# Shifting SBUF places to multiples of 256 bytes in a twelve-stage network kernel

## Chip, core and metric

The kernel runs on one core of a Trainium2 chip. The metric is device time in microseconds (us) of one execution; lower is better. A difference of about 0.3% (8 us) is the least that a measurement of this kernel can tell from none.

## The reference

A residual stream `x` of 256 tokens by 1024 features passes through twelve blocks in float32. In short:

```python
for i in range(2):                                  # first block
    x = x + 0.5 * swiglu(rmsnorm(x, g), w_in, w_out)
    x = x + (chunked_sgu(h) if i == 0 else pool_mixer(h))
    x = x + 0.5 * swiglu(rmsnorm(x, g), w_in, w_out)
x = rmsnorm(x, final_norm)
x = x + gt1 * rms_norm(attention(h) @ w_o)          # second block
x = x + gt2 * rms_norm(moe_ffn(h2))                 # 32 experts, top 4
x = x + rms_norm(merged @ w_out)                    # third block: attention + state space
x = x + rms_norm(memory_cross_attention(h))
x = x + rms_norm(conv_ffn(h))

def moe_ffn(h, ...):                                # for every expert e with its tokens
    hid = xb @ w_mlp1[e] + b_mlp1[e]                # 1024 x 2048 weights, 8 MiB
    act = clipped_swiglu(hid)
    y   = act @ w_mlp2[e] + b_mlp2[e]               # 1024 x 1024 weights, 4 MiB
```

The 32 experts' weights are 12 MiB each, 384 MiB together.

## The kernel before

**Dense stages.** A weight column block of 128 outputs is loaded by one DMA of 1 MiB (128 partitions, 8 KiB each) into a place `raw` (pool `rawp`, ten places, `slot` and `raw`, lines 311 to 318). ACT casts it to a float32r tile `hi` (line 181), DVE subtracts to get `lo` (line 182); `parts` (line 327) takes the two from a ring of places of 8 KiB in the pools `splitp` and `splitr`. The inputs are split the same way (`input`, `ahi`/`alo` and others). `mm3` (lines 198 to 200) then makes three products for every 128 inputs: hi with hi, hi with lo, lo with hi, each with a 128x128 stationary operand and 256 moving columns. These are the "split products".

**Experts' stage** (`moe`, line 1270 on). The weights are not split. `weights` (line 1299) issues twelve DMAs of 1 MiB for each expert on SP's queue (`load`, line 1294): eight parts of `w_mlp1`, four of `w_mlp2`, each 128 rows of 8192 bytes. They go round a cycle of sixteen places (line 1285): seven `raw`, four `wb` from the pool `p3` (`own`, line 1281), the two places that are lent to it, `input` and the residual `xT` itself (line 1284), then three `raw`. So a load begins as soon as the product that last read its place is done, and up to sixteen loads run ahead. `xT` is saved to DRAM first (`kept`, line 1342) and read back at the end. `xe` holds the rows of the tokens that an expert gets; its place is lent to one load of the first expert. First layer products are at lines 1516 and 1548 (stationary `xe`, moving a weight place), second layer at 1590.

**How places are laid out.** A pool is a stretch of SBUF that opens on top of the pools still open, on the left or the right end; what a pool holds is laid out in it in order, at multiples of 32 bytes. `shift(pool, n)` (line 90) only reserves n bytes that nothing uses; it issues no instruction. Where a new pool covers what an earlier one held, the first writer of each new tile waits for the last reader of every old tile it overlaps. As allocated in the kernel before (start address modulo 256, and modulo 512 where it matters): `xT`, `raw`, `input` at 224; `wb` and `xe` at 32; the `hi`/`lo` places at 32; the moving operands of the split products at 224, which is 192 behind the stationary ones modulo 512, or 320 ahead. `wb` stands exactly on the four places that `splitp` held before the stage, and `b1`, `quarter`, `halves` and `xe0` exactly on the fifth.

**Order of issue.** Instructions are put in order by a scheduler that goes by priorities and by when operands are ready; inside `in_order` blocks PE follows the program. SP works through its DMAs strictly in that order, so a DMA that waits for its place holds up all that stand behind it. The last products ahead of the experts belong to a side job that is interleaved with attention and the experts (`mem.key(6)`, line 1188).

Of the kernel before, what the change touches and what calls it, by code (L numbers as in the profile page):

```python
# [41 lines left out]
class Net:  # L42
    def __init__(self, ctx, tc, I):
        self.ctx, self.tc, self.nc, self.I = ctx, tc, tc.nc, I
        self.uid = 0
        pool = lambda name, bufs, **kw: ctx.enter_context(tc.tile_pool(name=name, bufs=bufs, **kw))
        self.const = pool("const", 1)
        self.psum = pool("psum", 8, space=PSUM)
        self.small = pool("small", 2)
        self.rawp = pool("rawp", 10, reuse_waits="tile")  # L50
        self.inputs = pool("inputs", 2, reuse_waits="tile")
        self.ring_size, self.ring_scope, self.right_scope, self.latest = None, None, None, ()
        self.rings(8)
        nc = self.nc
        self.ident = self.const.tile([P, P], F32, name="ident")
        make_identity(nc, self.ident)
        self.ones = self.const.tile([P, 1], F32, name="ones")
        nc.vector.memset(self.ones, 1.0)
        self.mhalf = self.const.tile([P, 4], F32, name="mhalf")
        nc.vector.memset(self.mhalf, -0.5)  # L60
        self.sc = self.const.tile([P, KT], F32, name="sc")
        self.xT = self.const.tile([P, KT, T], F32, name="xT")
        self.new_inputs()

# [4 lines left out]
    def rings(self, split, right=0, left=0):  # L69

        if self.right_scope is not None:
            self.right_scope.close()
        self.right_scope = ExitStack()
        if self.ring_size != split:
            if self.ring_scope is not None:
                self.ring_scope.close()
            self.ring_size = split
            self.ring_scope = ExitStack()
            if split:
                self.splitp = self.ring_scope.enter_context(self.tc.tile_pool(name=self.nm("splitp"), bufs=split, reuse_waits="tile"))  # L80
        self.turn_of = [self.splitp] * split
        self.shifts = {}
        for n, side in ((right, "right"), (left, "left")):
            if n:
                more = self.right_scope.enter_context(self.tc.tile_pool(name=self.nm("splitr"), bufs=n, reuse_waits="tile", side=side))
                self.turn_of += [more] * n
                if side == "right":
                    self.shifts[more] = 448

    def shift(self, pool, n):  # L90

# [1178 lines left out]
    def moe(self, V, mod, router, w1, w2, b2, nxt, ahead, mem):  # L1270
# [7 lines left out]
        top, p0, p6 = (pool(name, side="right") for name in ("mot", "mo0", "mo6"))  # L1278
        p3, pb = pool("mo3", 4), pool("mob")

        own = lambda: p3.tile([P, 2048], F32, tag="wb", name=self.nm("wb"))


# [1593 lines left out]
```

## Time and profile before

| what | value |
|---|---|
| median of 3 runs | 2651.24 us (2647.99 to 2656.15) |
| the profiled execution | 2649.92 us |
| its span, first to last instruction | 2648.2 us |
| mean granted TensorE clock | 0.95 |
| PE, DVE, ACT, POOL busy | 91%, 51%, 35%, 10% |
| DMA over the span | 718.30 MB, mean 271 GB/s |

The profile is of one execution; the times of its rows add up to the span, and 1.7 us lie around it. Busy PE time is modelled from pipelined matmuls, so a busy PE is not PE at its peak; counts of matmuls per stretch (the x behind a busy time) tell its pace. "DMA" is the mean busy share of 16 DMA engines. Times in rows count from the start of the span.

### The profile page before, as it was taken

The page shows a single profiled execution, that of the slowest core. Times are in us where ns is not written, and L with a number is a line of the kernel's source. Part 1 is how long each engine was busy: PE and PEld are TensorE (multiplying, and loading weights), DVE is VectorE, ACT ScalarE, POOL GpSimd, SP SyncE. Part 2 cuts the span into 40 slices and gives each one's busy share as a digit, 9 for nine tenths or more (in the row PEclk, how much of TensorE's full clock was granted, in tenths as well). Part 3 has the DMA queues.
Part 4 walks back from the last instruction along what each step waited for, and adds up shares of the span by engine and source line. Part 5 has one row for each costly group of instructions (what it writes and reads, how often), then busy time and mean ns, then how long its engine had stood idle before and what let it go on. Part 6 is the DMA issues. An engine that isn't in the chain of part 4 may idle for free. (4 is left out here: it accounts for less than half of the span.)

```text
span 2648.2 us, 42809 instructions
## 1 busy us (share of the span) xinstructions
PE 2416.1 (91%) x17207; PEld 1833.3 (69%) x17207; DVE 1339.3 (51%) x2778; ACT 915.4 (35%) x1531; POOL 254.3 (10%) x444
## 2 busy tenths in 40 slices
PE   7999999999999998999988988888787688999998
PEld 7998999999989998783333433233232156899997
DVE  5556767577787766832112111111111059766875
ACT  4446454454454445531101101001010043555653
POOL 0011000110021003120000000000000027111000
PEclk9999999999999999989989999899898788999998
DMA  8965555676647652469999999999999973444640
GB/s 247 329 196 193 185 204 192 220 263 231 216 158 248 223 168 94 158 250 391 419 414 417 416 416 419 420 419 419 420 419 420 420 286 112 160 165 139 222 144 17
DMA packets 274405, 718.30 MB, mean 271 GB/s; under 512 B 15055, under 2 KB 179387, under 8 KB 223643
## 3 DMA queue, kind: packets, MB, share of 16 engines
q1 hardware_dynamic: 269658, 705.73, 71.3%
q0 software_dynamic: 4544, 9.80, 1.1%
q8 instruction: 136, 2.23, 0.3%
q14 instruction: 67, 0.54, 0.1%
HBM read 704.89 MB, written 10.59 MB: 270 GB/s over the span
## 5 line engine op out<-in xcount | busy, mean ns | idle before, releaser
L200 PE MATMUL b<-input,hi 128*128 128x256 f32 x2392 | 671.6, 281 | 16.2 <-DVE hi L182 16.1
L198 PE MATMUL b<-input,hi 128*128 128x256 f32 x2392 | 675.5, 282 | 6.4 <-ACT input L210 5.1
L182 DVE TENSOR_TENSOR hi<-raw,hi 128x1024 fp32r<-128x1024 f32 (+3 forms) x517 | 605.8, 1183 | 146.4 <-ACT hi L181 145.5
L199 PE MATMUL b<-input,hi 128*128 128x256 f32 x2392 | 670.6, 280 | 3.7 <-DVE input L211 2.4
L181 ACT CAST hi<-raw 128x1024 fp32r<-128x1024 f32 (+3 forms) x517 | 509.0, 1002 | 469.4 <-PE b L200 408.2
L198 PEld LDWEIGHTS b<-input,hi 128*128 128x128 f32 x2392 | 456.4, 191 | 20.1 <-ACT hi L181 7.2
L200 PEld LDWEIGHTS b<-input,hi 128*128 128x128 f32 x2392 | 455.4, 190 | 18.9 <-DVE hi L182 18.8
L199 PEld LDWEIGHTS b<-input,hi 128*128 128x128 f32 x2392 | 456.0, 191 | 5.8 <-DVE input L211 4.5
L1497 DVE TENSOR_SCALAR g<-b 128x256 f32<-128x256 f32 x48 | 20.3, 423 | 588.4 <-PE b L1516 327.7
L198 PE MATMUL b<-ahi,hi 128*128 128x256 f32 x1072 | 299.2, 280 | 2.2 <-ACT ahi L181 2.2
L199 PE MATMUL b<-alo,hi 128*128 128x256 f32 x1072 | 298.0, 278 | 3.3 <-DVE alo L660 1.9
L200 PE MATMUL b<-ahi,hi 128*128 128x256 f32 x1072 | 297.5, 278 | 0.8 <-DVE hi L182 0.8
L199 PEld LDWEIGHTS b<-alo,hi 128*128 128x128 f32 x1072 | 202.4, 189 | 4.4 <-DVE alo L182 2.2
L198 PEld LDWEIGHTS b<-ahi,hi 128*128 128x128 f32 x1072 | 202.0, 189 | 3.6 <-ACT ahi L181 3.6
L200 PEld LDWEIGHTS b<-ahi,hi 128*128 128x128 f32 x1072 | 202.0, 189 | 1.0 <-DVE hi L182 1.0
L1500 ACT ACTIVATE sg<-g 128x256 f32<-128x256 f32 x48 | 20.0, 417 | 516.8 <-DVE g L1497 516.8
L1548 PE MATMUL b<-raw,xe 128*64 128x512 f32 x600 | 140.9, 607 | 10.2 <-DMA raw<-in_w_mlp_dram 10.1
L1516 PE MATMUL b<-raw,xe 128*32 128x512 f32 x784 | 107.9, 660 | 32.9 <-DMA raw<-in_w_mlp_dram 32.9
L1597 ACT COPY y<-b 64x512 f32<-64x512 f32 x68 | 39.4, 580 | 253.9 <-PE b L1590 246.1
L474 DVE TENSOR_TENSOR t<-b,rb 128x256 f32<-128x256 f32 x88 | 37.1, 422 | 151.7 <-PE b L200 151.6
L1548 PEld LDWEIGHTS b<-raw,xe 128*64 128x64 f32 x600 | 39.8, 138 | 104.8 <-issue 73.8
L1516 PEld LDWEIGHTS b<-raw,xe 128*32 128x32 f32 x784 | 20.3, 113 | 106.6 <-DMA raw<-in_w_mlp_dram 67.8
(673 smaller groups left out, 3317.3 us busy)
## 6 DMA issues: line engine op xcount, KB each, us to landing
raw<-in_w_mlp_dram SPq DMA_DIRECT2D x241, 1024.0 KB
wb<-in_w_mlp_dram SPq DMA_DIRECT2D x96, 1024.0 KB
raw<-in_ffn_w_in_dram SPq DMA_DIRECT2D x84, 1024.0 KB
raw<-in_ffn_w_out_dram SPq DMA_DIRECT2D x44, 1024.0 KB
raw<-in_w_ada_dram SPq DMA_DIRECT2D x24, 1024.0 KB
input<-in_w_mlp_dram SPq DMA_DIRECT2D x23, 1024.0 KB
xT<-in_w_mlp_dram SPq DMA_DIRECT2D x23, 1024.0 KB
raw<-in_ffn_w_up_dram SPq DMA_DIRECT2D x22, 1024.0 KB
```

What stands on the lines that cost most here:

```text
L181: a = self.nc.scalar.copy(hi, src)
L182: return a.ins, self.nc.vector.tensor_tensor(lo, src, hi.bitcast(F32), op=ALU.subtract).ins
L198: mm(out, whi, xhi, start=start, stop=False, skip_group_check=True)
L199: mm(out, whi, xlo, start=False, stop=False, skip_group_check=True)
L200: mm(out, wlo, xhi, start=False, stop=stop, skip_group_check=True)
L474: nc.vector.tensor_tensor(t, ps[:, :T], rb, op=ALU.mult)
L1497: nc.vector.tensor_scalar(g, v[:, :, 0], 7.0, None, op0=ALU.min)
L1500: nc.scalar.activation(sg, g, AF.Sigmoid, scale=1.702)
L1516: mm(ps[32 * c:32 * c + 32, :], xe(k), chunk(w[k][:, 0, :], c), start=False, stop=k == KT - 1, tile_position=(0, 32 * c), skip_group_check ...
L1548: mm(pq[q][64 * b:64 * b + 64, :], xe(k), chunk(w[:, 0, :], 2 * q + b), start=False, stop=k == KT - 1, tile_position=(0, 64 * b), skip_gro ...
L1597: nc.scalar.copy(y[64 * z:64 * z + 64, 512 * c:512 * c + 512], py[64 * c:64 * c + 64, :])
```

## The change

Three lines. In `Net.__init__` 32 bytes are left free ahead of the residual, which moves every left-hand place behind it up by 32 bytes. In `rings` the gap in the right-hand ring shrinks by 32, so that this ring moves up by 32 as well. In `moe` 192 bytes are left free ahead of the `wb` places, so that they and all of the stage's left-hand places behind them move up by 224 in all.

```diff
@@ Net.__init__
         self.sc = self.const.tile([P, KT], F32, name="sc")
+        self.shift(self.const, 32)
         self.xT = self.const.tile([P, KT, T], F32, name="xT")
@@ Net.rings
                 if side == "right":
-                    self.shifts[more] = 448
+                    self.shifts[more] = 416
@@ Net.moe
         p3, pb = pool("mo3", 4), pool("mob")
 
+        self.shift(p3, 192)
         own = lambda: p3.tile([P, 2048], F32, tag="wb", name=self.nm("wb"))
```

By the layout, `xT`, `raw`, `input`, `wb` and `xe` then start at 0 modulo 256 (256 modulo 512); the `hi`/`lo` places start at 64, and the moving operands of the split products at 256, both modulo 512, as far apart as before. `wb` no longer stands on the old ring's places but 192 bytes behind their starts.

## Rows read from the trace of the kernel before

**Rows 1.** The page, parts 1, 2 and 5: engines; DMA in forty slices; costliest groups.

```profile
PE 2416.1 (91%) x17207; PEld 1833.3 (69%) x17207; DVE 1339.3 (51%) x2778; ACT 915.4 (35%) x1531; POOL 254.3 (10%) x444
...
DMA  8965555676647652469999999999999973444640
...
L198 PE MATMUL b<-input,hi 128*128 128x256 f32 x2392 | 675.5, 282 | 6.4 <-ACT input L210 5.1
...
L198 PE MATMUL b<-ahi,hi 128*128 128x256 f32 x1072 | 299.2, 280 | 2.2 <-ACT ahi L181 2.2
```

**Rows 2.** Windows: start:end us, length, busy us (instructions) by engine, PEclk, DMA share, GB/s.

```profile
300.00:400.00 100.00, 99.93 (x869) 99.35 (x868) 70.86 (x103) 52.31 (x77) 6.35 (x4) 1.00 0.59 200
...
600.00:700.00 100.00, 100.00 (x882) 98.44 (x882) 77.25 (x208) 45.11 (x61) 6.46 (x10) 1.00 0.71 237
...
1200.00:1300.00 100.00, 94.56 (x497) 41.41 (x500) 18.43 (x53) 12.09 (x24) 0.00 (x0) 0.98 0.99 406
...
1600.00:1700.00 100.00, 81.83 (x404) 29.99 (x403) 15.27 (x46) 8.61 (x17) 0.00 (x0) 0.93 1.01 420
```

**Rows 3.** SP's waits, 1200 to 2100 us: total us, times, longest us.

```profile
SPq L1294 <- DMA raw<-in_w_mlp_dram: 365.1, 193, 3.0
...
SPq L1294 <- PE b L1590: 21.6, 20, 7.6
```

**Rows 4.** DMA, 1121 to 1123.5 us: loads into `raw` alone.

```profile
DMA packets 145, 1.06 MB, mean 423 GB/s; under 512 B 16, under 2 KB 16, under 8 KB 16
...
q1 hardware_dynamic: 145, 1.06, 100.0%
```

**Rows 5.** DMA, 1149.5 to 1154 us: loads into `wb` alone.

```profile
DMA packets 261, 1.91 MB, mean 424 GB/s; under 512 B 28, under 2 KB 28, under 8 KB 28
...
q1 hardware_dynamic: 261, 1.91, 100.3%
```

**Rows 6.** DMA, 1600 to 1700 us: loads into places of both kinds.

```profile
DMA packets 5758, 41.97 MB, mean 420 GB/s; under 512 B 638, under 2 KB 638, under 8 KB 638
...
q1 hardware_dynamic: 5754, 41.91, 101.1%
```

**Rows 7.** The page, part 6: DMA issues into `wb`, their count and size.

```profile
wb<-in_w_mlp_dram SPq DMA_DIRECT2D x96, 1024.0 KB
```

**Rows 8.** Windows of 20 us of split products, columns as in rows 2.

```profile
69.50:89.50 20.00, 20.00 (x172) 20.00 (x172) 14.39 (x19) 10.70 (x15) 1.13 (x3) 1.00 1.06 374
629.50:649.50 20.00, 20.00 (x179) 20.00 (x178) 18.93 (x65) 8.36 (x11) 1.45 (x2) 1.00 0.62 209
```

**Rows 9.** Line 1516's matmuls by moving place: duration ns min/median/max, first and last start.

```profile
L1516 PE MATMUL b<-raw,xe x784: 592/592/1063, 1247.8 to 2108.5; 128*32 128x512 f32 x196
L1516 PE MATMUL b<-wb,xe x320: 592/592/1062, 1242.7 to 2118.5; 128*32 128x512 f32 x160
```

**Rows 10.** SP's timeline, 1140 to 1175 us: start us, us, what.

```profile
1145.51 1.28 SPq L1294 DMA_DIRECT2D wb<-in_w_mlp_dram  x3
1158.54 0.33 SPq L1342 DMA_DIRECT2D kept<-xT  x1
1162.87 0.32 SPq L1344 DMA_DIRECT2D b<-b  x1
1163.23 0.42 SPq L1294 DMA_DIRECT2D wb<-in_w_mlp_dram  x1
1163.71 0.42 SPq L1294 DMA_DIRECT2D xe<-in_w_mlp_dram  x1
1171.10 0.36 SPq L1294 DMA_DIRECT2D input<-in_w_mlp_dram  x1
```

**Rows 11.** SP's waits, 1140 to 1175 us: total us, times, longest us.

```profile
SPq L1294 <- PE b L200: 13.8, 1, 13.8
...
SPq L1344 <- PE b L200: 3.9, 1, 3.9
```

**Rows 12.** DVE's timeline, 2125 to 2156 us: first split after the experts.

```profile
2134.69 2.36 DVE L182 TENSOR_TENSOR hi<-raw,hi 128x1024 fp32r<-128x1024 f32 x2 [12.49 <-ACT hi L181]
```

## The prediction

> **What bounds the kernel now.** I read the page first: PE is busy for 91% of the span, DMA shows 9 in every slice of a block in the second half [rows 1]. So there are two regimes, and the windows tell them apart [rows 2]. [...] In the experts' stage DMA is: from 1200 us on it is busy at 0.99 to 1.01 and moves 406 to 420 GB/s, while PE has gaps (81.83 us busy in 1600 to 1700, clock 0.93). SP's waits there are for earlier loads to land, 365.1 us behind those into `raw` alone, against 21.6 us for the largest on a product [rows 3]: places come free before the queue needs them. The stage's length is therefore 384 loads of 1 MiB at the pace of the wire: 1,048,576 bytes at 420 GB/s is 2.50 us, times 384 is 959 us, 36% of the span. What could matter is the pace of these loads, the pace of a split product in the rest, and when the stream of loads starts.
>
> The sum below is against the profiled execution, 2649.92 us, which lies 1.3 us under the median of 2651.24; I add the change in us to the median.
>
> **1. The pace of the loads.** The change adds and removes no transfer; it moves the SBUF end of every load. The trace has no load that ends on a multiple of 256, but two other positions: `raw` at 224 and `wb` at 32. Loads into `raw` alone: 145 packets, 16 of them the 4-byte ones that signal, at 100.0% of 16 engines for 2.5 us, that is 40 us over 129 large packets, the small ones' share left in: 310 ns each, 423 GB/s [rows 4]. Into `wb` alone: 100.3% of 16 engines for 4.5 us is 72.2 us, over 233 large packets 310 ns, 424 GB/s [rows 5]. The two positions cost the same. In the steady stage, with both kinds mixed, it is 101.1% of 1600 us over 5754 - 638 = 5116 large ones: 316 ns, 420 GB/s [rows 6]. So the 6 ns that the stage pays over the short stretches do not follow the position, and I take 0. Bounds: if aligned places brought the stage from 420 to the 424 GB/s of rows 5, it would lose 959 x 4/424 = 9 us; nothing excludes a loss of the same size, so +9 us is the other end.
>
> [...]
>
> **2. The split products.** `hi`/`lo` and their moving operands all go up by 32, so their distance stays. What a product costs today varies by itself: 20 us with PE wholly busy at clock 1.00 hold 172 matmuls in one place and 179 in another, 116.3 and 111.7 ns each [rows 8]; over 100 us it is 113.4 ns (882 in 100 us) and 115.0 ns (869 in 99.93 us) [rows 2]. Both paces occur at one and the same offsets, so the offset alone doesn't set them. I take 0. Bounds: the page's groups of lines 198 to 200 hold 3 x (2392 + 1072) = 10,392 split products, of PE's 17,207 [rows 1]. Half way between the two windows of rows 2 is 114.2 ns. All of them at 113.4 would be 10,392 x 0.8 ns = 8 us faster; all at 116.3 would be 10,392 x 2.1 ns = 22 us slower.
>
> **3. The experts' products.** `xe` and the places move relative to each other: `raw` stood 192 ahead of `xe` modulo 512, `wb` at 0, and after the change all at 0. Line 1516 takes a median of 592 ns with either [rows 9], and PE isn't the bound there; 0, and were one slower, its cover is the DMA queue's backlog, PE's 18 us of gaps per 100 [rows 2].
>
> **4. When the stream starts.** This is the one term that I can price from the code. `wb` stood exactly on the four places of the ring that attention leaves; pushed up by 192, each `wb` now also covers the first 192 bytes of the next one, and the last of them reaches into the fifth place, on which `b1` stands. Today three `wb` loads go at 1145.51 to 1146.8, after a wait of 13.8 us for split products [rows 10, 11]. `b1` waits 3.9 us more for the last split product on the fifth place and goes at 1162.87 [rows 10, 11]. By the layout the second of the three `wb` loads then waits for that same product. If the scheduler, which orders by readiness, puts it behind `b1`, one load more stands behind 1162.87. There are today 2.5 loads (`b1` is half a one, `wb`, `xe`): 6.2 us, done at 1169.1 at the earliest, against the issue of the next at 1171.10. That leaves a slack of 0 to 2.0 us, so that a load more costs 0.5 to 2.5 us, 1.5 in the middle. If the order stays, the second and third `wb` and the copy of `xT` stand behind it too: 5.5 loads, 13.8 us, done at 1176.7, 5.6 us after 1171.10. Lower end 0: the stage's own stalls (406 GB/s at 1200 to 1300 against 420 later [rows 2]) can swallow it. Since all later loads run back to back, a late start is carried to the end. I take +1.5.
>
> **5. All else.** Where the stage ends, the new ring again lies across two `wb` each. Their last reader starts at 2118.5 us [rows 9], DVE's part of the first split into the ring at 2134.69 [rows 12]: 16 us of cover, less ACT's part before it, 0. No engine's queue gets an instruction; ACT, DVE and POOL (35%, 51%, 10% busy [rows 1]) keep theirs.
>
> **Sum:** 0 + 0 + 0 + 1.5 + 0: profiled 2651.4, median 2652.7, say **2653 us**, +0.06%, well inside the 0.3% (8 us) that a measurement of this kernel can tell from no change.
>
> **The rivals.**
> - *The loads get shorter.* For: the stage is nothing but loads, and no row shows one at a multiple of 256. Against: 310 ns at 224 and at 32. By rows, 9 us off: 2644; twice that, were the steady packets to go as far below the short stretches' pace as they now stand above it: 2635. Chance 0.14.
> [...]
> - *The split products settle at their quick pace* because rows begin on a boundary. For: two paces exist. Against: one offset shows both. 8 us off: 2645. Chance 0.12.
> - *The split products settle at their slow pace.* Same place, lines 198 to 200: whichever way operand reads fall against the loading of the next weights may depend on where both begin. It decides from 0.8 ns a product (8 us over 10,392) and costs up to 22 us: 2675. Against: the distance stays. Chance 0.13.
> - *The start slips further*, order kept and other places late as well: 5.6 us and up, 2657 to 2661. Chance 0.07.
> - *The places don't move as said.* The shifts are only reserved bytes, and later pools follow; by the layout they do move. It would look like no change.
>
> **How the numbers follow.** No change (with the small wait) has 0.50. Faster by over 0.3%: 0.14, 0.04 and 0.12, 0.30 together. Slower: 0.13 and 0.07, 0.20. The forecast's own range is 2645 to 2659. To leave out no more than 2 in 10 it goes down to 2634, where the shorter loads at twice the row's gain lie, and up to 2666, over half of the slow pace; beyond lie the 29 us and the full 22 us.
>
> **What would show it.** Right: the experts' windows at 419 to 420 GB/s and about 316 ns a large packet; 870 to 882 matmuls per 100 us in the dense stages; one `wb` load behind `b1`, and the stage's first full stretch within 2 us of where it was. Wrong: 424 GB/s or more from 1200 to 2100 us; counts of 885 and up, or 860 and down, in dense windows at clock 1.00; SP holding `kept` until after 1163 us.

## The result, and the profile after

| what | before | after |
|---|---|---|
| median of 4 runs, us | 2651.76 | 2635.2 (2632.54 to 2638.02) |
| ratio to before | | 0.994 (95% interval 0.9927 to 0.9952) |
| the profiled execution, us | 2649.92 | 2632.54 |
| its span, us | 2648.2 | 2630.9 |

The change makes the kernel about 16 us faster, 0.6%, twice what can be told from no change. The prediction said no change, 2653 us. Where did the time go? First the page of the kernel before, part 2's last row (GB/s in forty slices of the span) and part 3's largest queue; then the same two rows of the kernel after, with its engines.

```profile
GB/s 247 329 196 193 185 204 192 220 263 231 216 158 248 223 168 94 158 250 391 419 414 417 416 416 419 420 419 419 420 419 420 420 286 112 160 165 139 222 144 17
...
q1 hardware_dynamic: 269658, 705.73, 71.3%
```

```profile
PE 2409.1 (92%) x17207; PEld 1836.2 (70%) x17207; DVE 1338.7 (51%) x2778; ACT 915.5 (35%) x1531; POOL 253.0 (10%) x444
...
GB/s 244 336 195 200 184 203 192 225 263 233 215 153 256 221 174 93 154 224 408 427 421 425 425 424 427 426 427 426 427 426 427 425 249 112 172 173 143 202 145 17
...
q1 hardware_dynamic: 269658, 705.73, 70.0%
```

Packets and bytes of the queue are the same to the last digit, and so are the engines' instructions. But where the kernel before sat at 414 to 420 GB/s in the slices of the experts' stage, the kernel after sits at 421 to 427. The windows put that into stages (columns as in [rows 2]); kernel after:

```profile
300.00:400.00 100.00, 99.93 (x870) 99.35 (x869) 71.32 (x112) 51.43 (x76) 6.35 (x4) 1.00 0.58 200
600.00:700.00 100.00, 100.00 (x882) 98.44 (x882) 77.26 (x215) 45.00 (x62) 6.46 (x10) 1.00 0.66 227
1200.00:1300.00 100.00, 91.35 (x480) 37.50 (x478) 16.81 (x48) 10.91 (x22) 0.00 (x0) 0.98 1.00 414
1600.00:1700.00 100.00, 80.93 (x413) 30.95 (x414) 15.42 (x47) 9.73 (x19) 0.00 (x0) 0.91 1.01 427
```

The split products are untouched: 870 and 882 in the two dense windows, against 869 and 882 [rows 2]. The experts' stage has 427 GB/s where it had 420, with the DMA engines just as busy: each packet takes less time. The DMA view of the same stretch, kernel after, answers to [rows 6]:

```profile
DMA packets 5855, 42.68 MB, mean 427 GB/s; under 512 B 649, under 2 KB 649, under 8 KB 649
...
q1 hardware_dynamic: 5849, 42.60, 100.9%
```

100.9% of 1600 us over 5849 - 649 = 5200 large packets is 310 ns each, the small ones' share left in; before it was 316. The large packets' own durations in the trace, averaged over some 35,000 of them between about 1290 and 1990 us, say it more closely: **315.46 ns before, 309.85 ns after**. 5.6 ns over 384 loads of 8 rows on each of 16 engines (3072 rows an engine) is 17.2 us. And the stage is shorter by that order; line 1518 (1516 before) of the kernel after, with first and last start:

```profile
L1518 PE MATMUL b<-raw,xe x784: 592/592/1062, 1242.6 to 2088.0; 128*32 128x512 f32 x196
...
L1518 PE MATMUL b<-wb,xe x320: 592/592/1062, 1237.4 to 2097.8; 128*32 128x512 f32 x160
```

From the first product on `wb` to the last it is 860.4 us, against 875.8 (1242.7 to 2118.5) in [rows 9]: 15.4 us less. What is left of the 17.4 us between the two profiled executions lies elsewhere: the stage begins 5.3 us earlier, and behind it 3.3 us are lost again. Both go with the clock that the throttle granted. Here are two long dense windows, before and then after:

```profile
0.00:1100.00 1100.00, 1062.58 (x8834) 1019.72 (x8835) 773.25 (x1600) 534.92 (x828) 122.63 (x233) 0.98 0.63 207
...
2200.00:2630.00 430.00, 406.94 (x3292) 389.52 (x3292) 328.79 (x528) 224.55 (x368) 78.99 (x121) 0.96 0.42 141
```

```profile
0.00:1100.00 1100.00, 1064.43 (x8867) 1020.58 (x8868) 778.74 (x1619) 538.82 (x842) 122.42 (x233) 0.99 0.61 209
...
2200.00:2630.00 430.00, 398.88 (x3202) 382.97 (x3200) 314.28 (x509) 222.97 (x367) 66.21 (x108) 0.94 0.40 138
```

PEclk is 0.98 and 0.96 before, 0.99 and 0.94 after (the second window holds other work, as the kernel after is some 20 us ahead there, so only its clock compares). The earlier start isn't the change's: run e1 below, in which no load's place begins on a multiple of 256, has the same in its trace, with PEclk 0.99, as many matmuls by 1100 us, and its first product on `wb` at 1236.7 us against 1237.4.

```profile
0.00:1100.00 1100.00, 1064.35 (x8873) 1020.17 (x8873) 778.87 (x1621) 538.60 (x842) 122.98 (x234) 0.99 0.63 209
```

The 3.3 us at the end are chance of one execution too, as far as the traces tell: behind the last product on `wb` they have 528.5 (e3) to 535.0 us (e6), and 529.7 before and 533.1 after lie between.

The dense stages' packets became shorter as well, which hardly shows in time. 71.3% of 2648.2 us is 1888 us of queue time an engine, 70.0% of 2630.9 is 1842: 46 us less, of which the experts' rows are 17. The other 29 us gave no time that can be told; PE is the bound there, busy for 1062.58 of the first 1100 us before and 1064.43 after. Up to 1100 us a packet of 1 KiB took 50.8 ns before, 50.5 in e1 and 48.8 after, and yet e1 starts its experts' stage as early as the kernel after.

### The profile page after: what moved, and what is told of

Its sections match the earlier page's. It is cut to its first block, busy times and chain, and to the rows that moved or that the text cites. A ratio compares the mean times of both kernels' runs of the same rounds, so it can differ in the third digit from the quotient of the medians.

```text
span 2630.9 us, 42809 instructions
## 1 busy us (share of the span) xinstructions
PE 2409.1 (92%) x17207; PEld 1836.2 (70%) x17207; DVE 1338.7 (51%) x2778; ACT 915.5 (35%) x1531; POOL 253.0 (10%) x444
## 5 line engine op out<-in xcount | busy, mean ns | idle before, releaser
L201 PEld LDWEIGHTS b<-input,hi 128*128 128x128 f32 x2392 | 457.7, 191 | 17.3 <-DVE hi L183 17.2
```

The source lines that it names most:

```text
L201: mm(out, wlo, xhi, start=False, stop=stop, skip_group_check=True)
```

## The experiments

Four theories stood at the start: A, a row pays when it begins off a multiple of 256; B, what costs is that loads to places of different residue (224 and 32) are in flight together; C and D, as A with multiples of 64 or of 128. All places are named by their start modulo 256, and each ratio is to runs of the kernel before on the same chip. "Row" is the mean duration of a row of 8192 bytes, taken as above. Runs e1 to e9 in one table:

| run | raw, input, xT | wb, xe | row, ns | GB/s, 1600 to 1700 | median, us | ratio to before (95% interval) |
|---|---|---|---|---|---|---|
| before | 224 | 32 | 315.46 | 420 | 2651 | |
| after | 0 | 0 | 309.85 | 427 | 2635.2 | 0.994 (0.9927 to 0.9952) |
| e1 | 64 | 64 | 314.53 | 421 | 2645.26 | 0.9977 (0.9967 to 0.9988) |
| e2 | 128 | 128 | 314.44 | 421 | 2646.47 | 0.9981 (0.997 to 0.9991) |
| e3 | 224 | 0 | 313.47 | 422 | 2643.03 | 0.9975 (0.9964 to 0.9987) |
| e4 | 0 | 32 | 310.13 | 427 | 2634.03 | 0.993 (0.9913 to 0.9948) |
| e5 | 32 | 32 | 315.53 | 420 | 2653.23 | 1.0007 (0.9995 to 1.0018) |
| e6 | 224 | 224 | 315.67 | 420 | 2649.92 | 0.9997 (0.9988 to 1.0007) |
| e8 | 32 | 0 | 313.41 | 422 | 2644.63 | 0.9973 (0.9962 to 0.9985) |
| e9 | 0 | 64 | 310.05 | 427 | 2632.8 | 0.9932 (0.9918 to 0.9946) |

The time follows the row: 3.07 us for each ns. e8's 2.05 ns make 6.3 us (measured 6.7), e9's 5.41 ns make 16.6 us (18.6), e5's none (+1.9, the interval holds none). A median also holds where the stage begins, which varies by itself, in the traces from 1236.7 (e1, e9) to 1244.5 us (e6). The stage alone, from the first to the last product on `wb`, takes 875.8 us before, 877.3 in e5 and e6, 873.9 and 873.4 in e1 and e2, 872.0 and 870.9 in e3 and e8, 862.0 and 861.6 in e4 and e9, 860.4 after.

**e1 and e2: the same layout, further up.**

```diff
-        self.shift(self.const, 32)
+        self.shift(self.const, 96)          # e2: 160
-                    self.shifts[more] = 416
+                    self.shifts[more] = 352     # e2: 288
```

> All places of the change stand 64 bytes further up, at 64 modulo 256 (xT, raw, input, wb, xe alike); hi/lo and the moving operands move with them, 320 bytes apart as ever. The after kernel's gain lies in the experts' stage: a row of 8192 bytes took 309.9 ns on the mean there against 315.5 before. Theory A (a row pays when it begins and ends off a multiple of 256): rows stay near 315 ns, 420 GB/s, the time is the before kernel's, 2651 us within 3. Theory B (it costs only while loads to places of different residue are in flight together, as 224 and 32 were): all are equal here, so 309 to 310 ns, 427 GB/s, about 2635 us. Theory C (any multiple of 64 is as good): the same as B, 2635 us. Theory D (multiples of 128 are needed): as A, 2651 us.

> All places of the change 128 bytes further up, at 128 modulo 256. Theory A (multiples of 256): near 315 ns a row, 420 GB/s, 2651 us within 3. Theory B (mixed residues): 309 to 310 ns, 427 GB/s, 2635 us. Theories C (64) and D (128): 2635 us as well. With the run at 64, C and D part: C has both at 2635, D only this one.

Rows of e1, then of e2 in the windows:

```profile
1600.00:1700.00 100.00, 80.88 (x404) 29.82 (x404) 16.76 (x50) 8.97 (x18) 0.00 (x0) 0.91 1.01 421
```

```profile
1600.00:1700.00 100.00, 80.86 (x406) 28.89 (x402) 15.96 (x47) 8.60 (x17) 0.00 (x0) 0.94 1.01 421
```

421 GB/s and 314.5 ns, all places alike: B, C and D fall; being all at one residue, or at a multiple of 128, doesn't bring the gain. A stands but for one ns, which the rows at 64 and 128 are quicker than those at 32 and 224 (e5, e6), and some 5 us of time, of which that ns makes 3; in the stage alone it is 2 against before and 3 to 4 against e5 and e6, and the rest goes with the earlier starts. Why these rows are quicker, no run tells.

**e3 and e4: one part of the loads each.** e3 is the kernel before with `self.shift(p3, 224)` alone; e4 is the change with 224 in the place of 192 there.

> The before kernel with only the wb places and what lies behind them moved, by 224, so that wb and xe stand at 0 modulo 256 and raw, input and xT stay at 224. 97 of the 384 loads are aligned. Theories A, C, D (each row pays for itself): 97/384 of the stage's 16 us, so about 4 us off, 2647 us, and in the steady stage the rows of wb near 309 ns and the others near 315, 421 to 422 GB/s. Theory B (mixed residues): nothing gained, 2651 us, 315 ns for both kinds. Against all of them stands a theory E (an unaligned row also slows the aligned ones that run beside it): rows of both kinds between 313 and 315 ns, 0 to 4 us.

> The change with the wb places pushed up by 224 instead of 192: raw, input and xT at 0 modulo 256, wb and xe at 32 as before. 287 of the 384 loads are aligned. Theories A, C, D: 287/384 of 16 us, about 12 us off, 2639 us, rows of wb near 315 ns and the others near 309. Theory B: nothing gained, 2651 us. Theory E: between, rows of both kinds above 309 ns, 4 to 12 us off. Together with e3 this is the dose: if the gain goes by the number of aligned loads, 4 and 12 add up to the 16 of the change.

e3, then e4:

```profile
1600.00:1700.00 100.00, 82.10 (x409) 31.07 (x412) 16.76 (x50) 8.97 (x18) 0.00 (x0) 0.91 1.01 422
```

```profile
1600.00:1700.00 100.00, 81.57 (x414) 31.13 (x411) 16.49 (x50) 10.13 (x20) 0.00 (x0) 0.91 1.01 427
```

The dose doesn't add up. With 97 loads aligned the time falls by 7 us and the row by 2.0 ns; with the other 287 the time falls by all of it and the row by 5.3 ns, 427 GB/s: 7.3 ns together, where all loads make 5.6. In e4 the unaligned quarter goes free. So A, as I had put it, falls with the sum. So does the theory E of the two expectations, that an unaligned row also slows the aligned ones beside it: it asked for 4 to 12 us in e4, which gave some 18. Either 32 is a free position, or an unaligned minority is carried by the aligned rows around it.

e3's trace shows which loads are carried. I take its rows in order, 128 to a load (so a load's edges are blurred by a few rows), and average each place of the cycle from 1290 to 1990 us. The first `wb` after the unaligned loads has 312.7 ns a row, the other three 309.2 to 309.7. `input` right behind them, at 224, has 309.4 ns, `xT` 311.4, the next `raw` 312.9, and all others 314.0 and more. In the kernel before every one of these places has 314.6 or more.

**e5, e6, e8, e9: which of the two.** e5 is e1's edit with 64 and 384, e8 the same with `p3` at 160; e6 is the kernel before with `self.shift(p3, 192)`; e9 is the change without its third line.

> After e1 to e4: places all at 64 or at 128 keep 314.5 ns a row in the steady stage (before 315.5, after 309.9); raw, input and xT at 0 with wb at 32 has 310 for both kinds, and wb at 0 with the others at 224 has about 311 for wb and 315 for raw. Here all places stand at 32 modulo 256. Theory P (a row pays by its own position; 32 happens to be free, 224, 64 and 128 are not): 310 ns, 427 GB/s, 2635 us. Theory Q (a row off a multiple of 256 pays, but only where the loads ahead of it and behind it are off it too, so that a minority of them among aligned ones goes free): 314 to 315 ns, 420 to 421 GB/s, 2646 to 2651 us.

> The before kernel with only the wb places pushed up by 192, so that wb and xe stand at 224 like the others: nothing aligned, nothing mixed, and the new overlap of wb with the old ring's places is in as in the change. Theories P and Q: 315 ns a row, and the time of before within 4 us. If the mixing of 224 and 32 were the cost: 310 ns, 2635 us. If the overlap (the start of the stream) is worth anything by itself, it shows as the time against before: I expected +1.5 us, 0 to +5.6.

> The mirror of e4: wb and xe at 0, raw, input and xT at 32 modulo 256. Theory P (32 is free by itself): 310 ns for both kinds, 427 GB/s, 2635 us. Theory Q (the unaligned majority pays): wb near 310, raw 313 to 315, as in e3, 421 to 423 GB/s, about 2643 us.

> The change without its third line: raw, input and xT at 0 modulo 256, wb and xe at 64 and exactly on the old ring's places, as before the change. Three wb loads may then go before b1 again, at about 1140 us. Theory P (64 pays by itself, e1): wb rows near 314, the others 310, 425 to 426 GB/s, and 97/384 of the gain lost, about 2639 us. Theory Q (a minority goes free): 310 ns for both, 2635 us, and up to 5 us less if the three early wb loads shorten the start of the stage.

e5, then e9:

```profile
1600.00:1700.00 100.00, 82.08 (x406) 30.10 (x404) 15.12 (x46) 8.60 (x17) 0.00 (x0) 0.93 1.01 420
```

```profile
1600.00:1700.00 100.00, 82.31 (x413) 31.01 (x414) 15.00 (x46) 9.57 (x19) 0.00 (x0) 0.90 1.01 427
```

P falls: 32 for all is as slow as 224 for all (315.53 and 315.67 ns), and 64, slow by itself in e1, is free for a quarter of the rows in e9. Q holds in all four. For the design this says that the third line of the change isn't needed: e9 at 0.9932, e4 at 0.993 and the change at 0.994 can't be told apart, and none of the kernels tried is measurably better than these. e9's early loads (three `wb` at 1138.99 us, ahead of `b1` at 1156.19) gave nothing that can be measured.

e6 also holds the answer to why the kernel before didn't show the cost in the stretches I read. Behind `b1`, at 1164.07 us, five loads to 224 start out of a pause. The DMA view of e6 from 1166.7 to 1171.7 us, and then from 1175 to 1180 us:

```profile
DMA packets 300, 2.14 MB, mean 428 GB/s; under 512 B 33, under 2 KB 33, under 8 KB 45
...
q1 hardware_dynamic: 300, 2.14, 101.6%
```

```profile
DMA packets 285, 2.08 MB, mean 416 GB/s; under 512 B 31, under 2 KB 31, under 8 KB 31
...
q1 hardware_dynamic: 284, 2.07, 100.4%
```

These first 5 us run at the pace of aligned rows, 428 GB/s, with not one row aligned; the rows' own durations turn from 309 ns to 313 and more at about 1173 us, and soon after the pace is 416 (100.4% of 80 us over 253 large packets of the queue, 317 ns). In e6 the cost of an unaligned row came only after some 6 us of unbroken stream (1166.7 to about 1173 us).

**e10 and e11: shorter rows.** In both kernels each load goes as two DMAs of 128 rows of 4096 bytes.

```diff
-            nc.sync.dma_start(t, src)
+            for z in range(2):
+                i = (slice(None), slice(None), slice(1024 * z, 1024 * z + 1024)) if n == 2048 else (slice(None), slice(z, z + 1))
+                nc.sync.dma_start(t[i], src[i])
```

> The before kernel with every load of the experts' stage issued as two DMAs, each with 128 rows of 4096 bytes instead of 8192; both halves begin at the same residue as before (224 or 32). A row of 4096 bytes took 159 ns where nothing slowed it, so 8 KiB cost 318 ns instead of 309 by themselves, 8 ns more, about 25 us over 384 loads (8 rows on each of 16 engines, 8 ns each). Theory per row (an unaligned row pays some 5.6 ns whatever its length): 164.5 ns a row, 329 ns per 8 KiB, 42 us above before, about 2693 us, 403 GB/s. Theory per byte (1.8% of the row): 162 ns a row, 324 ns per 8 KiB, 25 us above before, about 2676 us, 409 to 410 GB/s.

> The same edit on the changed kernel (rows of 4096 bytes at 0 modulo 256). Both theories: 159 ns a row, 318 ns per 8 KiB, 25 us above the changed kernel, about 2660 us, 415 GB/s. The distance to e10 is what tells: 33 us if an unaligned row pays a fixed sum, 16 us if it pays by the byte. If the two DMAs cost something else (issue on SP, completion), both runs carry it.

Measured 2679.11 us (1.0093, 1.0075 to 1.0111) and 2657.0 us (1.0018, 1.0005 to 1.0031). The DMA view of 1300 to 2000 us, e10 and then e11:

```profile
DMA packets 80232, 284.20 MB, mean 406 GB/s; under 512 B 8644, under 2 KB 11716, under 8 KB 80188
...
q1 hardware_dynamic: 79948, 282.85, 102.0%
```

```profile
DMA packets 82342, 291.89 MB, mean 417 GB/s; under 512 B 8879, under 2 KB 11951, under 8 KB 82297
...
q1 hardware_dynamic: 82057, 290.53, 102.1%
```

The rows' own durations average 163.87 ns against 159.86, 4.0 ns apart; the times are 22.1 us apart, where a fixed sum per row asked for 33 and a cost by the byte for 16. Both miss. A third length is in the traces: behind the experts, loads with rows of 1 KiB (into `raw`, from `turns` and `in_w_in_dram`, the same two sources in both kernels) fill the queue for some us. Kernel before, 2158 to 2168 us, then after, 2138 to 2142 us:

```profile
DMA packets 3454, 3.50 MB, mean 350 GB/s; under 512 B 48, under 2 KB 3453, under 8 KB 3453
...
q1 hardware_dynamic: 3453, 3.49, 108.4%
```

```profile
DMA packets 1522, 1.54 MB, mean 385 GB/s; under 512 B 17, under 2 KB 1522, under 8 KB 1522
...
q1 hardware_dynamic: 1522, 1.54, 108.6%
```

That is 50.9 and 46.2 ns a row, 4.7 ns apart. So an unaligned row costs 5.6, 4.0 and 4.7 ns at 8, 4 and 1 KiB, and what it spends them on stays open. In the short row it is a tenth.

**e12 and e13: the aligned loads spread out.** e12 is e3 with another cycle of places from the second round on, e13 the kernel before with the same cycle.

```diff
-        places = itertools.cycle([self.slot] * 7 + [own] * 4 + lent + [self.slot] * 3)
+        three, two = [self.slot] * 3 + [own], [self.slot] * 2
+        places = itertools.chain([self.slot] * 7 + [own] * 4 + lent + [self.slot] * 3,
+                                 itertools.cycle(three + three + two + lent[:1] + [own] + lent[1:] + two + [own]))
```

> e3 (wb at 0, raw, input and xT at 224) with the cycle of places in another order from the second round on: one aligned wb after every three unaligned places, instead of four wb in a row. Theory of a backlog (an unaligned row writes for longer than it is read, the lag is hidden up to some depth and is worked off during aligned rows): each wb buys free passage for at least one of the three, so at most 8 of 16 loads pay, 312.7 ns a row on the mean or less (e3 313.5), 309 ns rows mixed in everywhere. Theory of a state (the stream is either free of it or not, by the majority): 315 ns, hardly below before, with wb no quicker than the others.

> The control to e12: the before kernel (224 and 32) with the same new order of places. Every theory of position: 315.5 ns a row in the steady stage, 419 to 420 GB/s; if the order by itself changed the pace of the loads, it would show here.

e12 took 2656.92 us (1.0014, 1.0004 to 1.0023), e13 2661.01 in a single run, with 313.43 and 315.36 ns a row. e12:

```profile
1200.00:1300.00 100.00, 93.21 (x474) 41.73 (x474) 19.32 (x55) 12.18 (x24) 0.00 (x0) 0.98 0.91 378
1600.00:1700.00 100.00, 86.25 (x427) 33.77 (x430) 14.29 (x43) 8.77 (x17) 0.67 (x1) 0.96 1.01 422
```

The new order costs time where it sets in (378 GB/s at 1200 to 1300, 378 in e13 as well), which hides its pace in the median; the pace is e3's to 0.04 ns, 422 GB/s, and the control's is that of before. Both theories of e12 miss their numbers. The theory of a state asked for 315; the backlog as I had sized it, each aligned load letting at least one other pass, for 312.7. But that the order doesn't matter and only the share of aligned rows does is what a backlog has to give, once its size is taken from e3. As an estimate from the rows' means, four aligned loads of 16 and twelve at 315.5 make 313.47 on the mean if an aligned one works at (16 x 313.47 - 12 x 315.5) / 4 = 307.4 ns. An aligned row then makes up 309.9 - 307.4 = 2.5 ns, not 5.6 or more. With the shares turned round it is (12 x 307.4 + 4 x 315.5) / 16 = 309.4 ns, under the 309.9 that a row takes anyway: e4 and e9 go free. One number, taken from e3, agrees with e4, e8, e9 and e12 (310.13, 313.41, 310.05 and 313.43 ns). It was sized after these runs, e8 and e12 only repeat e3's share, no run was made to test it, and none shows a backlog itself. But the loads of e3 that go free bear it out: as an estimate, four aligned loads, 32 rows on each engine, make up 32 x 2.5 = 80 ns, which pays for some 14 rows at 5.6 ns, nearly two loads of 8 rows, and about that much goes free behind them (`input` 309.4 ns, `xT` 311.4). And the some 6 us of e6 are 19 rows on each engine, a lag of 19 x 5.6 = 106 ns before it shows: more than the 80, so by this account it makes no difference whether the aligned loads come together or apart.

## Why the prediction was wrong

**Step 1 failed**, at "The two positions cost the same" and "So the 6 ns that the stage pays over the short stretches do not follow the position, and I take 0." Three things were wrong in it:
- The two positions, 224 and 32, are both off a multiple of 256. That they cost the same is true, to 0.14 ns (e5, e6), and says nothing of a position on one.
- 310 ns in the stretches of [rows 4, 5] was read as the price of an unaligned row. They last 2.5 and 4.5 us, and in e6 a stream out of a pause ran at the aligned pace, 428 GB/s, for some 6 us before the price showed (416 GB/s). The 316 ns of [rows 6] were the price.
- The 6 ns between them were seen and left without a cause. They were the whole gain: 5.6 ns a row, 17.2 us by rows, 15.4 in the stage. The lower bound of 9 us was too near also by the prediction's own rows: it took the 424 GB/s of a short stretch for the pace, while the 6 ns, on 3072 rows an engine, are 18 us. The stage came to 427 GB/s.

Of the rivals, "the loads get shorter" (0.14) was right in what happens. That its second figure, 2635, was met is luck: it asked for steady rows as far below the 310 ns of the short stretches as they now stood above, and they went to 309.85. The figure fits because the 9 us that it doubles were half of what 6 ns make. The 0.04 and the 29 us beyond the range stand for a saving of 1 part in 33 of every packet's time, and no run shows that term: the row of 8 KiB lost 5.6 of its 315.46 ns, 1 part in 56, that of 4 KiB 4.0 of 163.87 and that of 1 KiB 4.7 of 50.9.

**Step 2** (split products, 0) was right: 870 and 882 in the dense windows, with PE busy for 99.93 and 100.00 of their 100 us. **Step 3** (experts' products, 0) too: 592 ns in line 1518 on `raw` and `wb`. **Step 4** (start of the stream, +1.5) was right that the overlap holds `wb` loads back behind `b1`, and not in how many. SP's timeline, kernel after, answers to [rows 10]:

```profile
1152.47 0.33 SPq L1344 DMA_DIRECT2D kept<-xT  x1
1156.71 0.32 SPq L1346 DMA_DIRECT2D b<-b  x1
1157.08 2.13 SPq L1296 DMA_DIRECT2D wb<-in_w_mlp_dram  x4
1159.25 0.46 SPq L1296 DMA_DIRECT2D xe<-in_w_mlp_dram  x1
1165.44 0.36 SPq L1296 DMA_DIRECT2D input<-in_w_mlp_dram  x1
```

All four `wb` loads stand behind `b1`, three more than before, where I had reckoned with one. What they cost is too little to be told. e6, which has this overlap and nothing aligned, has the same order and takes 0.9997 of before (0.9988 to 1.0007), 2 us at the upper end; its stage is 1.5 us longer than that of before, while that of the kernel after is 1.2 us shorter than that of e9, which keeps the old order. From `b1` to the first product on `wb` it is 79.8 us before and 80.7 after. The late loads find room in the stream: the 80 us from `b1` on, before and then after,

```profile
1162.87:1242.87 80.00, 73.82 (x352) 39.25 (x356) 24.35 (x103) 13.25 (x29) 6.36 (x36) 0.91 0.93 369
```

```profile
1156.71:1236.71 80.00, 75.70 (x347) 41.64 (x347) 23.25 (x102) 13.24 (x29) 6.48 (x36) 0.87 0.98 402
```

Before, the DMA engines had gaps there (a share of 0.93); the late loads fill them (0.98). **Step 5** (all else, 0): the profile shows nothing against it. The sum missed by its first term, and the sign named for that, 424 GB/s or more, came: 426 on the mean of 1300 to 2000 us (423 to 427 in windows of 100 us), though 414 in the first, 1200 to 1300.

## What to carry to other kernels

Where a stage is nothing but DMA into SBUF, look at one packet's duration in the steady stream and beside it at the shortest one of that size anywhere in the trace: the few ns between them here, 316 against 310, were a cost with a cause, rows that began off a multiple of 256 bytes (1.8% of the stage). A quiet stretch of a few microseconds didn't price this stream (424 GB/s over 4.5 us, 420 in the steady stage); take the price from a stretch as long and as full as the one that it is for. Most of the places were enough: with three rows of four aligned the rest went free (310.13 ns in e4, 310.05 in e9), and one of four bought about a third of the gain (2.0 of 5.6 ns, e3).

## What the runs showed of the hardware that was not expected

- An unaligned row cost nothing in the first 6 us or so of a stream out of a pause (309 ns and 428 GB/s, then 317 ns and 416, in e6).
- Aligned rows carried unaligned ones: 310 ns for all at three quarters aligned (e4, e9), 313.4 to 313.5 at one quarter (e3, e8, e12), whatever the order. Why, no run shows; in e3 it is the loads right behind the aligned ones that go free (309.4 ns in `input`, against 314.0 and more in the places further behind).
- Which residue it is hardly mattered: 32 and 224 cost 5.7 to 5.8 ns (e5, e6), 64 and 128 cost 4.6 to 4.7 (e2, e1). That ns stays open. All aligned places of these runs stand at 256 modulo 512; no run has another multiple of 256.
- The cost per row was near the same for short rows, 4.0 and 4.7 ns at 4 and 1 KiB against 5.6 at 8, so it weighed more there: 350 against 385 GB/s with rows of 1 KiB, where the queue was full.
- 1 ns of DMA pace in a row of 8 KiB is worth 3.07 us here, while 29 us of queue time saved in the dense stages were worth nothing that the start of the experts' stage shows (e1).
